# Causal mask products first in the score banks, q and k features one step apart, and modulation dots in the first halves of the down stages

## The chip, the cores and the metric

The kernel runs on one core of a Trainium2 chip. The metric is the device time of one execution in microseconds (us). Before the change the median of three runs is 1501.16 us (1500.08 to 1504.64).

The core has five engines that run side by side and wait for each other by semaphores: PE (matrix products into PSUM banks; its weight loads are listed apart as PEld), DVE and ACT (element-wise work), POOL and SP (here they mostly issue DMAs).

## What is computed

A trunk of two layers over 512 tokens of width 1024, all in f32. In each layer, with `h` the normalised and modulated input:

```python
mod = c_act @ w_ada + b_ada                      # shifts, scales and gains of both halves
h = rmsnorm(x, norm1_w) * (1 + sc1) + sh1
u = h @ w_in                                     # pool, conv, q, k, v and three gates
merged = gate0 * (pool(u) @ p_pool) + gate1 * (conv(u) @ p_conv) + gate2 * (attn(q, k, v) @ p_attn)
x = x + g1 * (merged @ w_out)
h2 = rmsnorm(x, norm2_w) * (1 + sc2) + sh2
x = x + g2 * ((silu(h2 @ w_gate) * (h2 @ w_up)) @ w_down)
```

The attention has 8 heads of 64 with normalised q and k and a partial rotation. Keys lie in two blocks of 256. A query sees the causal part of its own block, and queries of the second block see the first block unless its gate rules it out.

## The kernel before, in words

**Products in three passes.** Every f32 operand is split into a high part and a rest (`split_w` for weights, L320 to L330, ACT line L325 and DVE line L328; `split_from` for activations, L504 to L513). A product is three matrix products, high x high, high x rest, rest x high (`mm3`, L157). `matmul`, `transpose` and all that is wrapped in `pin` keep the program's order on their engine; the rest of ACT's and DVE's work is put in order by the framework's planner.

**The clock of the program.** `mm3` counts the columns of main products. Every 2048 columns (four `mm3` of 512) it calls `tick` (L133): each fiber (a generator) whose count has run out goes one step further, and then `run_bulk` adds `bulk_rate` to a credit that is capped at 4.0 and runs queued side tasks as long as the credit isn't negative, each taking its cost off.

**Weights.** They arrive by SP's queue as raw tiles, in the order in which they are used (`load_w`, `next_w`; usually four chunks ahead, two in the second half of a down stage).

**Attention** (L645) is a fiber. For each of four head pairs it transposes and splits the q and the k features (`to_features`, L563: four transposes into one of the four PSUM banks with tag `mm`, then ACT L511 and DVE L512), both in one step, and starts four units, one for each block of 128 queries. A unit (L574) makes the scores of two heads in a PSUM tile `pair` (three passes, and the causal mask as a product of an identity with a bf16 mask, added after the first pass), the softmax (DVE L592 to L617, ACT L595 to L612), and some steps later the transposes of the probabilities (L624) and the product with v (L631), which is copied by ACT L637 and DVE L638. The gate products of the layer run meanwhile; the first product that needs the attention's result stands 56.5 steps after the conv products at which the fiber is queued.

**Norms.** `Norm.stat` sums squares by a product with ones; `newton` (L463) makes the reciprocal root: an ACT approximation (L467) and one Newton step in four DVE instructions (L468 to L471). It is called for halves of 256 columns, twice for each of three norms. `apply` then writes the tiles that the next products read (L479, L481, L482).

**Feed-forward.** It goes in four parts (`PARTS`, L47). In a part, hidden columns are computed singly or as pairs of columns by `glu_pair` (L1028), which saves products by sums of weight blocks. The sums are made by POOL's accumulating DMAs (L254, L256) and by DVE (L262, L263) in tiles of tag `w4`, of which there are six; a pair holds four. Each part ends in a down stage: eight output tiles of `nk` `mm3` each, added to x by L937.

**Modulation.** The vector c times `w_ada` is not made on PE. Each 128 outputs are one DMA of 512 KB (`ada_step`, L393, the load L395) and one DVE instruction with an accumulator (`ada_dot`, L371). The 16 dots that the second layer needs first are queued as side tasks at the end of the first part's GLU pairs (L1104), at a cost of 1.2 each, and their tiles are of tag `w4` too.

Of the kernel before, what the change touches and what calls it, by code (L numbers as in the profile page):

```python
# [17 lines left out]
ALU = mybir.AluOpType  # L18
# [3 lines left out]
P = 128  # L22
D = 1024
S = 512
L = 2
KT = D // P
# [12 lines left out]
EPS = 1e-6  # L39
# [38 lines left out]
def hybrid_trunk(ctx, tc, xT, ws, ada, cols, pool_w, qk_w, crow, pos, con, out):  # L78
    nc = tc.nc
    V, A, T = nc.vector, nc.scalar, nc.tensor  # L80
# [17 lines left out]
    def tmp():  # L98
        return work.tile([P, S], F32, tag="tmp", name=nm("tmp"), bufs=5)

    def ps_mm():
        return psum.tile([P, S], F32, tag="mm", name=nm("mm"), bufs=4)

    def ps_pair():
        return psum.tile([P, 2, S], F32, tag="pair", name=nm("pair"), bufs=2)
# [14 lines left out]
    bulk_rate, credit = [0.0], [0.0]  # L120
# [27 lines left out]
    def matmul(*a, **k):  # L148
        tc.keep_in_program_order(T.matmul(*a, **k))  # L149
# [48 lines left out]
    ident16 = const.tile([P, P], BF16, name="ident16")  # L198
# [240 lines left out]
    class Norm:  # L439
# [23 lines left out]
        def newton(self, lo, hi, bank):  # L463
            n = hi - lo
            ss = bank[:, lo:hi]
            y, v, t = tmp(), tmp(), tmp()
            A.activation(y[:, :n], ss, AF.Abs_reciprocal_sqrt, bias=epst, scale=1.0 / D)  # L467
            V.tensor_scalar(v[:, :n], ss, 1.0 / D, EPS, op0=ALU.mult, op1=ALU.add)  # L468
            V.tensor_mul(t[:, :n], v[:, :n], y[:, :n])
            V.scalar_tensor_tensor(t[:, :n], t[:, :n], -0.5, y[:, :n], op0=ALU.mult, op1=ALU.mult)  # L470
            V.scalar_tensor_tensor(self.rstd[:, lo:hi], t[:, :n], 1.5, y[:, :n],  # L471
                                   op0=ALU.add, op1=ALU.mult)
            self.y = y
# [100 lines left out]
    def unit(hp, i, q, k, v, y, nrq, prq):  # L574

        w = P * (i + 1)
        wm = max(w, BLOCK)
        s = ps_pair()
        for z, (qa, ka) in enumerate(((0, 0), (0, 1), (1, 0))):
            for a in range(2):  # L580
                r = slice(a * HD, (a + 1) * HD)
                matmul(s[:, a, :wm], q[qa][r, i * P:(i + 1) * P], k[ka][r, :wm],
                       start=(z == 0), stop=(z == 2))
            if z == 0:
                for a in range(2):
                    matmul(s[:, a, i * P:w], ident16, mask, start=False, stop=False)
        cell = lambda: sm([P, 2], tag="asm", bufs=16)
        nsc, sc = nrq[:, i, 2 * hp:2 * hp + 2], prq[:, i, 2 * hp:2 * hp + 2]
        m, nb, den = cell(), cell(), cell()
        pr = [tmp() for _ in range(2)]  # L590
        if w <= BLOCK:
            V.tensor_reduce(m, s[:, :, :w], axis=AX.X, op=ALU.max)  # L592
            V.tensor_mul(nb, m, nsc)
            for a in range(2):
                A.activation(pr[a][:, :w], s[:, a, :w], AF.Exp, bias=nb[:, a:a + 1],  # L595
                             scale=sc[:, a:a + 1], accum_out=den[:, a:a + 1])
        else:

            gs, pen, mp, nbp, d2 = cell(), cell(), cell(), cell(), cell()
            V.tensor_reduce(gs, s[:, :, :BLOCK], axis=AX.X, op=ALU.add)  # L600
            V.tensor_mul(gs, gs, sc)
            V.tensor_scalar(pen, gs, NEG * BLOCK * SCALE, NEG, op0=ALU.is_lt, op1=ALU.mult)
            V.tensor_reduce(mp, s[:, :, :BLOCK], axis=AX.X, op=ALU.max)
            V.tensor_add(mp, mp, pen)
            V.tensor_reduce(m, s[:, :, BLOCK:w], axis=AX.X, op=ALU.max)
            V.tensor_max(m, m, mp)
            V.tensor_mul(nb, m, nsc)
            V.tensor_add(nbp, nb, pen)
            for a in range(2):
                A.activation(pr[a][:, :BLOCK], s[:, a, :BLOCK], AF.Exp, bias=nbp[:, a:a + 1],  # L610
                             scale=sc[:, a:a + 1], accum_out=den[:, a:a + 1])
                A.activation(pr[a][:, BLOCK:w], s[:, a, BLOCK:w], AF.Exp, bias=nb[:, a:a + 1],  # L612
                             scale=sc[:, a:a + 1], accum_out=d2[:, a:a + 1])
            V.tensor_add(den, den, d2)
        V.reciprocal(den, den)
        for a in range(2):
            V.tensor_scalar(pr[a][:, :w], pr[a][:, :w], den[:, a:a + 1], None, op0=ALU.mult)  # L617
        yield WAIT[i]
        ph, pl = w4([P, i + 1, 2, P], F32R), w4([P, i + 1, 2, P], F32R)
        for aa in ([0, 1],) if i < 2 else ([0], [1]):  # L620
            tp = ps_mm().rearrange("p (j a q) -> p j a q", a=len(aa), q=P)[:, :i + 1]
            for a in aa:
                for j in range(i + 1):
                    transpose(tp[:, j, a - aa[0], :], pr[a][:, j * P:(j + 1) * P], ident)  # L624
            dst = (slice(None), slice(None), slice(aa[0], aa[-1] + 1))
            A.activation(ph[dst], tp, AF.Copy)  # L626
            V.tensor_sub(pl[dst], tp, f32(ph)[dst])
        yield 2
        po = ps_mm()
        for j in range(i + 1):  # L630
            mm3(po[:, :2 * P], cut(v[hp // 2][j // 2], slice(None), j % 2, slice(hp % 2 * P, (hp % 2 + 1) * P)),  # L631
                (ph[:, j].rearrange("p a q -> p (a q)"), pl[:, j].rearrange("p a q -> p (a q)")),
                j == 0, j == i, main=False)
        c = slice(i * P, (i + 1) * P)
        for a in range(2):
            r = slice(a * HD, (a + 1) * HD)
            A.activation(y[0][r, c], po[r, a * P:(a + 1) * P], AF.Copy)  # L637
            V.tensor_sub(y[1][r, c], po[r, a * P:(a + 1) * P], f32(y[0])[r, c])  # L638
# [6 lines left out]
    def attention(l, qk, v, nrq, prq, y_attn):  # L645

        for hp in range(PAIRS):
            q, k = to_features(l, qk, 0, hp), to_features(l, qk, 1, hp)
            y = bigt(), bigt()
            y_attn.append(y)  # L650
            yield 2
            for i in range(TT):
                start(unit(hp, i, q, k, v, y, nrq, prq))
                if i < TT - 1:
                    yield GAP[i]
            yield 1
# [45 lines left out]
    for l in range(L):  # L702
# [371 lines left out]
        for part, (along, single, pairs) in enumerate(PARTS):  # L1074
            act = []
            nk = along + single + 2 * pairs
            if along:
                held = {}
                for n, (k, lo, hi) in enumerate(HALVES + REST):
                    if n == 1:  # L1080
                        second(norm, l, 1, bank)
                        table(AF.Silu, norm.y[:, 0:1])
                    if k not in held:
                        held[k] = next_w()
                    for z in range(2 * FA):
                        mm3(f_ps[z][:, lo:hi], wblk(held[k], z), cut(norm.k(k), slice(None), slice(lo, hi)),
                            k == 0 and lo == 0, k == KT - 1)
                    if k >= HK:
                        make_forms(k - HK)
                del held  # L1090
                for z in range(FA):
                    glu(f_ps[z], f_ps[FA + z])
            for _ in range(single):
                wg = next_w()
                g = ps_mm()
                feature_tile(g, wg)
                u = ps_mm()
                feature_tile(u, next_w())
                glu(g, u)
            bulk_rate[0] = 0.0  # L1100
            for _ in range(pairs):
                glu_pair()
            if part == 0 and l + 1 < L:
                bulk.extend(ada_tasks(l + 1, (SC1, SH1)))  # L1104
            bulk_rate[0] = 0.75
            blk = Blocks(nk, 4)
            if part + 1 < len(PARTS):
                for n in range(KT):
                    o = ps_mm()
                    for k in range(nk):  # L1110
                        mm3(o, blk(n, k), act[k], k == 0, k == nk - 1)
                    residual(n, o, 0, S, G2)
            elif l + 1 == L:
                tail(lambda k: act[k], blk, G2, nk, None, True)
            else:
                flush_bulk()
                drain()
                n1 = Norm()
                table(AF.Abs_reciprocal_sqrt, f32(act[-1][1])[:, 0:1])
                scratch = ps_pair()  # L1120
                bank = scratch[:, 1]
                tail(lambda k: act[k], blk, G2, nk, n1, False, lead(n1, l + 1, 0, bank), 4)
                norm = n1
# [100 lines left out]
```

## Time and profile before

| What | Value |
|---|---|
| median of the runs | 1501.16 us |
| profiled execution, time | 1503.53 us |
| profiled execution, span of its instructions | 1501.7 us |
| mean granted clock of PE | 0.997 |
| HBM read | 213.65 MB |
| POOL busy | 105.6 us, 7% |

The profile is one execution. A line of the trace names the engine, the line of the kernel (L149 is the helper that records all products, so there one goes by tiles), the operation, and what is written and read (`mm<-big,whi`). A line of waits says which engine stood idle, at which of its lines, until which engine's which line was done: total, number of times, longest.

### The profile page before, as it was taken

Reading aid. Unit: us, or ns where it says so; the run is one execution under the profiler, and the core shown is the slowest. Engines: PE = TensorE matmul, PEld = TensorE weight load, DVE = VectorE, ACT = ScalarE, POOL = GpSimd, SP = SyncE. Lnnn points to the kernel's source line nnn. Section 1 sums busy time; section 2 is a strip of 40 time slices with the busy share of each in tenths; the row PEclk is TensorE's granted clock in tenths of the full one; section 3 lists DMA queues with packets and bytes.
Section 4 is the critical chain, followed back from the end, with each engine's and each line's share of the span. In section 5 each row is a group of like instructions: output and inputs, shape, how many; then the busy total and the mean of one; then the engine's idle time right before and its main releaser. Section 6 shows DMA issues by size and latency. Waiting matters only on the chain.

```text
span 1501.7 us, 22027 instructions
## 1 busy us (share of the span) xinstructions
PE 1478.1 (98%) x8523; PEld 1282.1 (85%) x8523; DVE 1042.0 (69%) x1797; ACT 657.7 (44%) x1138; POOL 105.6 (7%) x157
## 2 busy tenths in 40 slices
PE   9999999999999999999999999999999999999999
PEld 7887777788889898989988877777888889989997
DVE  7876777756586766767575678776666847757672
ACT  4634444433364352535444344554335534525350
POOL 0000000010000220310000000001000102211200
PEclk9999999999999999999999999999999999999999
DMA  9523434483226775644333244346721445727431
GB/s 343 194 85 140 155 128 140 146 237 130 64 99 210 216 185 175 175 114 133 107 104 100 98 155 140 134 133 187 226 82 53 126 141 148 199 80 195 137 99 71
DMA packets 84409, 217.20 MB, mean 145 GB/s; under 512 B 10832, under 2 KB 23760, under 8 KB 84304
## 3 DMA queue, kind: packets, MB, share of 16 engines
q1 hardware_dynamic: 67456, 177.37, 35.1%
q0 software_dynamic: 16128, 37.76, 11.4%
q8 instruction: 67, 1.10, 0.3%
q10 hardware_dynamic: 720, 0.66, 0.1%
q14 instruction: 38, 0.31, 0.1%
HBM read 213.65 MB, written 2.10 MB: 144 GB/s over the span
## 4 chain that ended last, share of the span: by engine, by line
PE 83%; DVE 6%; DMA 5%; ACT 3%; issue 2%; SPq 1%; POOL 0%; DVEq 0%; ACTq 0%; POOLq 0%
PE mm L149 70%; PE pair L149 11%; DMA raw<-in_ws 2%; DVE wlo L328 2%; PE mm L155 2%; DMA w<-in_ada 1%; ACT whi L325 1%; DMA w<-in_ws 1%; DVE w L371 1%; DVE raw L371 1%; SPq L232 0%; ACT tmp L610 0%; DMA x<-in_xT 0%; DMA raw<-in_ada 0%; ACT tmp L612 0%
## 5 line engine op out<-in xcount | busy, mean ns | idle before, releaser
L149 PE MATMUL mm<-big,whi 128*128 128x512 f32 (+1 forms) x4362 | 1085.7, 340 | 11.3 <-DVE tmp L1059 5.1
L149 PEld LDWEIGHTS mm<-big,whi 128*128 128x128 f32 x4362 | 748.6, 190 | 101.7 <-DVE tmp L1059 6.9
L149 PE MATMUL mm<-big,wlo 128*128 128x512 f32 (+1 forms) x2181 | 738.2, 338 | 0.0
L149 PEld LDWEIGHTS mm<-big,wlo 128*128 128x128 f32 x2181 | 415.1, 190 | 44.4
L325 ACT ACTIVATE whi<-raw 128x1024 fp32r<-128x1024 f32 (+2 forms) x240 | 248.9, 1039 | 334.9 <-PE mm L149 272.5
L328 DVE TENSOR_TENSOR wlo<-raw,whi 128x1024 fp32r<-128x1024 f32 (+2 forms) x240 | 285.7, 1195 | 121.5 <-ACT whi L325 116.2
L937 DVE SCALAR_TENSOR_TENSOR x<-mm,mod,x 128x512 f32<-128x512 f32 (+1 forms) x90 | 62.2, 691 | 121.5 <-PE mm L149 121.4
L325 ACT ACTIVATE whi<-w 128x1024 fp32r<-128x1024 f32 x72 | 76.2, 1058 | 148.9 <-PE mm L149 116.9
L254 POOL DMA_DIRECT2D w<-in_ws x72 | 45.5, 642 | 1027.1 <-issue 267.4
L328 DVE TENSOR_TENSOR wlo<-w,whi 128x1024 fp32r<-128x1024 f32 x72 | 86.8, 1222 | 30.5 <-ACT whi L325 29.8
L371 DVE SCALAR_TENSOR_TENSOR raw<-raw,csil 128x1024 f32<-128x1024 f32 x64 | 78.0, 1221 | 4.7 <-DMA raw<-in_ada 4.4
L149 PE MATMUL pair<-whi,big 128*128 128x512 f32 x224 | 76.8, 390 | 0.0
L149 PE MATMUL pair<-big,whi 128*128 128x256 f32 (+1 forms) x376 | 74.0, 295 | 0.0
L256 POOL DMA_DIRECT2D w<-in_ws x72 | 64.5, 920 | 131.7 <-DMA w<-in_ws 124.0
L149 PEld LDWEIGHTS pair<-big,whi 128*128 128x128 f32 x376 | 60.4, 191 | 2.2
L149 PE MATMUL mm<-whi,big 128*128 128x512 f32 x160 | 57.2, 394 | 1.7 <-ACT big L495 1.4
L149 PE MATMUL pair<-big,wlo 128*128 128x256 f32 (+1 forms) x188 | 55.4, 295 | 0.0
L509 DVE TENSOR_TENSOR big<-tmp,big 128x512 fp32r<-128x512 f32 x48 | 33.0, 691 | 24.9 <-ACT big L508 23.9
L149 PEld LDWEIGHTS pair<-whi,big 128*128 128x128 f32 x224 | 42.1, 188 | 8.6
L626 ACT ACTIVATE w<-mm 128x512 fp32r<-128x512 f32 (+2 forms) x48 | 24.0, 525 | 46.5 <-PE mm L155 46.5
L149 PE MATMUL pair<-wlo,big 128*128 128x512 f32 x112 | 43.7, 390 | 0.0
L371 DVE SCALAR_TENSOR_TENSOR w<-w,csil 128x1024 f32<-128x1024 f32 x32 | 38.5, 1222 | 5.7 <-DMA w<-in_ada 5.6
(185 smaller groups left out, 1265.6 us busy)
## 6 DMA issues: line engine op xcount, KB each, us to landing
raw<-in_ws SPq DMA_DIRECT2D x146, 512.0 KB, 3.4
w<-in_ws POOLq DMA_DIRECT2D x144, 256.0 KB, 5.0
raw<-in_ada SPq DMA_DIRECT2D x64, 512.0 KB, 3.4
w<-in_ada SPq DMA_DIRECT2D x32, 512.0 KB, 5.1
raw<-in_ws SPq DMA_DIRECT2D x64, 256.0 KB, 3.8
raw<-in_ws SPq DMA_DIRECT2D x24, 384.0 KB, 3.1
raw<-in_ws SPq DMA_DIRECT2D x16, 448.0 KB, 5.2
raw<-in_ws SPq DMA_DIRECT2D x36, 128.0 KB, 2.8
```

The source lines that it names most:

```text
L149: tc.keep_in_program_order(T.matmul(*a, **k))
L155: tc.keep_in_program_order(T.transpose(*a))
L254: nc.gpsimd.dma_start(dst, self.source(0, 1))
L256: nc.gpsimd.dma_start(dst, self.source(*other), accum_op=ALU.add)
L325: A.activation(hi[:, :n], raw[:, :n], AF.Copy)
L328: ins = V.tensor_sub(lo[:, :n], raw[:, :n], f32(hi)[:, :n])
L371: return V.scalar_tensor_tensor(aw, aw, 1.0, csil, op0=ALU.mult, op1=ALU.mult, accum_out=mod[l][:, part, j:j + 1])
L509: V.tensor_sub(lo, src, f32(hi))
L626: A.activation(ph[dst], tp, AF.Copy)
L937: V.scalar_tensor_tensor(x[k][:, lo:hi], src, mod[l][:, part, k:k + 1], x[k][:, lo:hi], op0=ALU.mult, op1=ALU.add)
```

## The change

Four edits. In `newton` the term `ss / D + EPS` is no longer made by an instruction of its own: three DVE instructions stand in place of four, and the first reads the PSUM bank and ACT's result. In `unit` the two mask products come first in the banks and start them, and all three score passes add to them. In `attention` the k features are made one step after the q features, so each head pair takes 12 steps in place of 11. In the down stages the credit rate is 1.5 a step in the first four of eight output tiles, and 0 in the last four of all parts but the last, where it was 0.75 throughout; only the first layer's down stages have tasks queued.

```diff
@@ -463,11 +463,10 @@
         def newton(self, lo, hi, bank):
             n = hi - lo
             ss = bank[:, lo:hi]
-            y, v, t = tmp(), tmp(), tmp()
+            y, t = tmp(), tmp()
             A.activation(y[:, :n], ss, AF.Abs_reciprocal_sqrt, bias=epst, scale=1.0 / D)
-            V.tensor_scalar(v[:, :n], ss, 1.0 / D, EPS, op0=ALU.mult, op1=ALU.add)
-            V.tensor_mul(t[:, :n], v[:, :n], y[:, :n])
-            V.scalar_tensor_tensor(t[:, :n], t[:, :n], -0.5, y[:, :n], op0=ALU.mult, op1=ALU.mult)
+            V.scalar_tensor_tensor(t[:, :n], ss, D * EPS, y[:, :n], op0=ALU.add, op1=ALU.mult)
+            V.scalar_tensor_tensor(t[:, :n], t[:, :n], -0.5 / D, y[:, :n], op0=ALU.mult, op1=ALU.mult)
@@ -576,14 +575,14 @@
         s = ps_pair()
+
+        for a in range(2):
+            matmul(s[:, a, i * P:w], ident16, mask, start=True, stop=True)
         for z, (qa, ka) in enumerate(((0, 0), (0, 1), (1, 0))):
             for a in range(2):
                 r = slice(a * HD, (a + 1) * HD)
                 matmul(s[:, a, :wm], q[qa][r, i * P:(i + 1) * P], k[ka][r, :wm],
-                       start=(z == 0), stop=(z == 2))
-            if z == 0:
-                for a in range(2):
-                    matmul(s[:, a, i * P:w], ident16, mask, start=False, stop=False)
+                       start=False, stop=(z == 2), skip_group_check=True)
@@ -645,7 +644,9 @@
         for hp in range(PAIRS):
-            q, k = to_features(l, qk, 0, hp), to_features(l, qk, 1, hp)
+            q = to_features(l, qk, 0, hp)
+            yield 1
+            k = to_features(l, qk, 1, hp)
@@ -1102,10 +1103,12 @@
             if part == 0 and l + 1 < L:
                 bulk.extend(ada_tasks(l + 1, (SC1, SH1)))
-            bulk_rate[0] = 0.75
+            bulk_rate[0] = 1.5
             blk = Blocks(nk, 4)
             if part + 1 < len(PARTS):
                 for n in range(KT):
+                    if n == KT // 2:
+                        bulk_rate[0] = 0.0
                     o = ps_mm()
```

## Prediction

> **What bounds the kernel now.** I read the page first: the shares of the engines, then who PE waits for, then PE's own starts in the stretches that the change touches.
>
> ```profile
> span 1501.7 us, 22027 instructions
> ## 1 busy us (share of the span) xinstructions
> PE 1478.1 (98%) x8523; PEld 1282.1 (85%) x8523; DVE 1042.0 (69%) x1797; ACT 657.7 (44%) x1138; POOL 105.6 (7%) x157
> ```
>
> PE is busy for 98% of the span and takes its instructions in the program's order, so only two things can move the time: the pace at which PE issues, and the 24 us in which it stands still. The profiled execution took 1503.5 us with a span of 1501.7, so 1.8 us lie around it; it is 2.4 us above the median of the three runs, 1501.16. The sum below is made against 1503.5. The waits of PE, longest in total first:
>
> ```profile
> PE mm L155 <- DVE tmp L617: 5.1, 4, 2.0
> PE mm L149 <- DVE tmp L1059: 5.1, 9, 2.9
> PE mm L149 <- DVE big L512: 2.8, 4, 1.4
> PE mm L149 <- ACT big L481: 2.4, 2, 1.2
> ```
>
> L617 ends the normalisation of an attention unit, L1059 is in a GLU pair, L512 splits q and k features, L481 is the first normalised tile after the Newton step. All three subjects of the change stand in this list, and the mask stands in none: its cost is hidden in PE's pace.
>
> **Part 1, mask products first.** One unit (the fourth kind, 512 columns), PE in order of time: start, length, what.
>
> ```profile
> 901.07 0.39 PE L149 MATMUL mm<-big,wlo 128*128 128x512 f32 x1
> 901.39 0.50 PE L149 MATMUL pair<-big,big 64*128 64x512 f32 x2
> 901.82 0.28 PE L149 MATMUL pair<-mask,ident 128*128 128x128 bf16 x2
> 902.03 0.73 PE L149 MATMUL pair<-big,big 64*128 64x512 f32 x4
> 902.70 0.88 PE L155 MATMUL mm<-ident,tmp 128*128 128x128 f32 x6
> ```
>
> A score pass is two products on 64 rows each, which run together. From the product ahead to pass 1: 0.32 us. From pass 1 to the mask: 0.43. The two mask products until pass 2: 0.21. Passes 2 and 3 until the transposes: 0.67, so 0.33 each. A full-height product of 512 columns otherwise makes way after 0.23:
>
> ```profile
> 177.70 5.47 PE mm L149 x24
> ```
>
> ```profile
> L149 PEld LDWEIGHTS <-ident 128*128 128x128 bf16 x64 | 3.6, 97 | 5.5 <-issue 3.4
> ```
>
> (5.47/24 = 0.228 us.) So the switch from full height to 64 rows costs 0.09 over the pace, and the switch from 64 rows back to the mask 0.10 over a pass (0.43 against 0.33), about the 97 ns of the mask's weight load, which starts only with its product.
>
> With the mask first, the row of steps is: product ahead to mask (X), mask to pass 1 0.21, then three passes of 0.33. The same instructions are issued; the saving is 0.32 + 0.43 - 0.33 - X = 0.42 - X. X isn't in the trace in this form. If the mask's weights are loaded under the product ahead, X is about the pace, 0.23; if they stand open, 0.23 + 0.097 = 0.32. The nearest row is the same switch to another full-height identity product, the transposes of q and k:
>
> ```profile
> 949.10 0.39 PE L149 MATMUL mm<-big,wlo 128*128 128x512 f32 x1
> 949.33 1.03 PE L155 MATMUL mm<-ident,w 128*128 128x128 f32 x8
> 951.76 0.50 PE L149 MATMUL mm<-big,whi 128*128 128x512 f32 x1 [1.40 <-DVE big L512]
> ```
>
> There X is 0.23, so I take it: 0.42 - 0.23 = 0.19 (0.184 with the pace unrounded). The mask row counts 64 loads, two a unit: 32 units. 32 x 0.184 = **-5.9 us**; ends: -2.9 (X = 0.32) and -6.1 (X = 0.225). Nothing hides it: PE itself gets shorter. The wait for q and k, and for the bank, stays where it is, ahead of the unit.
>
> The Trainium skill, "TensorE: Matmul & The Clock Gate", Part 3, The mechanism, speaks against this: a weight load is to overlap running products only where its row group differs. By it the mask's full-height load could not hide under a full-height product, and the part would give 2.9 us. The trace disagrees for other full-height loads (24 products at 0.228 us, each with a load of 0.19 of its own), but no run here shows it for the mask's type.
>
> **Part 2, q and k features one step apart.** A step is 2048 columns of main products, 12 x 0.227 = 2.7 us of PE. The rows of 949 show today's price: q's and k's eight transposes fill two of the four mm banks at once, the next product needs one of them back, and DVE comes to L512 late. PE's waits for L512 are the 2.8 us above. With the step between, q's bank has 2.7 us more until the next but one is asked for; k's transposes (0.44 us of PE), its ACT and DVE split (0.67 and 0.75) move by one step. No DMA moves with them. Gone then: between 0 and 2.8. The ring of four banks is asked as often, since k now meets the output of a unit in the same step, so I take three quarters, -2.1.
>
> Against it: the transposes of a fourth unit used to stand behind the next pair's first scores and now stand ahead of them.
>
> ```profile
> 260.30 0.38 PE L149 MATMUL pair<-big,big 64*128 64x256 f32 x2
> ...
> 261.26 1.09 PE L155 MATMUL mm<-ident,tmp 128*128 128x128 f32 x8
> ```
>
> ```profile
> 259.96 0.88 DVE L617 TENSOR_SCALAR tmp<-tmp,asm 128x512 f32<-128x512 f32 x2
> ```
>
> The normalisation ends at 260.84, the transposes start at 261.26: 0.42 us to spare, of which the scores fill 0.96. Without them this unit waits 0.5. Six units have a next pair; bounds 0 and 6 x 0.96 = 5.8; most have more to spare, so I take one more such unit, +1.0. **Part 2: -1.1 us**, ends -2.8 and +5.8. Four added steps also put the last unit's output at step 55 of the 56.5 that stand ahead of the first product with y_attn. What that product would wait for:
>
> ```profile
> 1050.07 1.59 PE L149 MATMUL mm<-w,big 128*128 128x256 f32 x12
> ```
>
> ```profile
> 1052.62 0.29 DVE L638 TENSOR_TENSOR big<-mm,big 64x128 fp32r<-64x128 f32 x1 [0.34 <-ACT big L637]
> ```
>
> The copies end 1.25 us after the output. After it 1.5 steps (4.1 us) are left, and three of that product's four terms come first: cost 0, and if DVE were busy for longer than that, the rest of its delay.
>
> **Part 3, the dots.** By the code's credit (4 at the start of a down stage, 1.2 a dot), the first down stage of layer 0 issues 4 dots in step 1 and 11 in its twelve steps now, 10 in its first six with the change; the second takes 6 in place of 5. The dots themselves aren't the limit, their tiles are:
>
> ```profile
> L371 DVE SCALAR_TENSOR_TENSOR w<-w,csil x11: 1218/1224/1227, 474.5 to 503.3; 128x1024 f32<-128x1024 f32 x11
> ```
>
> ```profile
> DMA to landing us min/median/max: 3.2/4.4/6.6
> ```
>
> ```profile
> 497.22 1.22 DVE L371 SCALAR_TENSOR_TENSOR w<-w,csil 128x1024 f32<-128x1024 f32 x1 [2.03 <-DMA w<-in_ada]
> ...
> 500.36 1.22 DVE L328 TENSOR_TENSOR wlo<-raw,whi 128x1024 fp32r<-128x1024 f32 x1
> 501.50 1.22 DVE L371 SCALAR_TENSOR_TENSOR w<-w,csil 128x1024 f32<-128x1024 f32 x1
> ...
> 504.44 0.75 DVE L937 SCALAR_TENSOR_TENSOR x<-mm,mod,x 128x512 f32<-128x512 f32 x1
> ```
>
> (The first row is the eleven dots of that stage, the second the landing of all 16 loads, the rest DVE at the stage's end.) Two w tiles are free for them, so two dots go every 5.6 us (a landing of 4.4 and a dot of 1.2). The ninth already waits for its DMA until 497.2 and can't come sooner. The tenth, loaded right behind, would run at 498.7 in place of 501.5, and there is no eleventh (at 503.3 now). So the tiles come free at 498.4 and 499.9, not at 502.7 and 504.5. What hangs on that (POOL, DVE, and two windows with length, busy time of PE, PEld, DVE, ACT and POOL, granted clock, DMA):
>
> ```profile
> 503.29 0.57 POOL L254 DMA_DIRECT2D w<-in_ws  x1 [47.22 <-DVE w L371]
> ```
>
> ```profile
> 505.11 3.48 DVE L328 TENSOR_TENSOR wlo<-w,whi 128x1024 fp32r<-128x1024 f32 x3
> ...
> 519.41 0.69 DVE L262 TENSOR_TENSOR w<-w,raw 128x512 f32<-128x512 f32 x1 [3.23 <-DMA w<-in_ws]
> ```
>
> ```profile
> 521.30:524.70 3.40, 0.63 (x5) 0.64 (x6) 3.04 (x6) 2.37 (x4) 0.43 (x1) 1.00 1.08 266
> 524.70:528.10 3.40, 3.40 (x18) 3.40 (x18) 2.87 (x5) 1.36 (x3) 1.55 (x3) 0.51 0.86 198
> ```
>
> POOL's sums for the second GLU pair wait for a dot's tile, land late, DVE stands still 3.23 us in L262 with L1059 queued behind it, and PE loses 2.9 us at L1059; after the window with 0.63 of 3.40 us busy the granted clock is 0.51 for 3.4 us, another 1.7. With the chain 4.3 us earlier at its start, and at least 2.5 in its second half, which runs over the three L328 (they can follow at 502.5, when the split of 500.36 is done behind the last dot), I take -2.7 for the wait and -1.7 for the clock: **-4.4 us**, ends 0 and -4.6. The denser loads pass SP's queue ahead of raw weights, and the split of 500.36 now stands behind all dots, at 501.3. Its weights are the GLU pair's, and the down stage before it lasts until 504.4 (the last L937), so 1.9 us cover it; were loads to take 3 us longer for a pair of dots, PE would lose about that.
>
> **Part 4, Newton.** One DVE instruction less in each of six. It matters only in the two where PE waits for L481:
>
> ```profile
> 400.99 0.42 DVE L468 TENSOR_SCALAR tmp<-pair 128x256 f32<-128x256 f32 x1
> ```
>
> ```profile
> 403.16 0.84 ACT L325 ACTIVATE whi<-raw 128x768 fp32r<-128x768 f32 x1 [2.21 <-PE mm L149]
> 403.91 0.49 ACT L481 ACTIVATE big<-tmp,mod 128x256 fp32r<-128x256 f32 x1
> ```
>
> DVE's chain gets about 0.42 shorter (the product that replaces it reads the same bank), but L481 stands in ACT's queue behind L325, which waits for PE. So **0**; if L481 came ahead of L325, at most its 0.84 each, -1.7 in all.
>
> **Sum:** -5.9 - 1.1 - 4.4 - 0 = -11.4, from 1503.5: 1492.1. The median run is 2.4 lower; if what it lacks is the clock drop, 9.7 come off it, 1491.5, and if it has the drop, 1489.8. I say **1491**.
>
> **Rivals.**
> 1. The mask's weight load stays open (X = 0.32): 3 us less, 1494. For: it is open now behind 64 rows. Against: the q/k transposes.
> 2. The banks' wait only moves, from q's and k's tiles to k's and the output's: -2.1 is lost, 1493. For: same four banks, DVE no freer; against: fewer asked for at once.
> 3. The dots don't get earlier: they run at the pace of two tiles whatever the credit says, and the tenth keeps its place behind L262 and L328. Then part 3 is 0: 1495.4. For: the ninth waits for DMA already; against: the last two dots came without a wait.
> 4. Slower: the shifted units meet DVE at worse moments, and L617 becomes the bound. Now 4 of the 16 third and fourth units wait, 1.28 us on the mean. If all 16 did, 12 x 1.28 = +15.4: 1506. It decides from about twelve more such units, each of which has to lose its slack first; that of the unit at 261.26 was only 0.42, which speaks for it, while the added step thins out DVE's work by a twelfth, which speaks against.
>
> **Chances.** Forecast 0.52 (1487 to 1495); rival 1 0.13, rival 2 0.13, rival 3 0.09, two of them together 0.05 (1498), rival 4 0.08. About 0.3%, 4.5 us, is what a measurement of this kernel can tell from no change, so faster means under 1496.7 and slower over 1505.7. Rivals 1 to 3 spill over 1496.7 with 0.03, 0.03 and 0.04, the pair with all: faster 0.77, same 0.16, slower 0.07. The range reaches from 1485 (all of 2.8 without the loss beside it, which is 1.7 more, Newton's 1.7, and another clock drop less) to 1499 (two rivals together).
>
> **What would show it.** Right: mask 0.23 after the product ahead and 32 units shorter by 0.18; no 3.2 us idle at L262 before the first pair's L1059, POOL's L254 near 498.5; L512 below 1 us among PE's waits. Wrong: a mask start 0.32 after the product ahead; a dot after 500 in the first down stage; L617's waits grown beyond 8 us.

## The result and the profile after

The changed kernel takes 1485.7 us in the median of four runs (1481.1 to 1487.2), beside 1502.3 for before on the same chip: a ratio of 0.9884, interval 0.9856 to 0.9911. Timed again later it gave 0.9869 (0.9847 to 0.9890). So it is 17 to 20 us faster; 10 were forecast, and 0.9884 of the 1501.16 shown then is 1483.7, just below the range that was given.

The profiled execution took 1481.1 us. Its span, and the busy time of its engines (us, share of the span, instructions):

```profile
span 1479.3 us, 22041 instructions
PE 1464.6 (99%) x8523; PEld 1276.7 (86%) x8523; DVE 1039.0 (70%) x1791; ACT 659.7 (45%) x1138; POOL 105.7 (7%) x157
```

PE issues the same 8523 products and is busy for 13.5 us less. Its waits (engine, its line, engine and line waited for, total, times, longest; L1060 is L1059 of before, and L616, L511, L480 and L481 each stand one lower than there):

```profile
PE mm L155 <- ACT whi L325: 2.6, 2, 1.7
PE mm L149 <- DVE tmp L1060: 2.2, 8, 0.3
...
PE mm L149 <- DVE big L481: 0.9, 4, 0.3
...
PE mm L149 <- ACT big L480: 0.4, 2, 0.2
PE mm L155 <- DVE big L511: 0.3, 1, 0.3
...
PE mm L155 <- DVE tmp L616: 0.2, 1, 0.2
```

The score waits (L617 and L512, 7.9 us) are down to 0.5, with 2.6 new ones at the units' transposes put down to L325 (whether that split was last there, or the unit's own normalisation beside it, the trace doesn't settle). The GLU wait lost 2.9, the Newton wait 1.1.

PE's own pace, a unit of 512 columns, first after:

```profile
934.27 0.39 PE L149 MATMUL mm<-big,wlo 128*128 128x512 f32 x1
934.50 0.28 PE L149 MATMUL pair<-mask,ident 128*128 128x128 bf16 x2
934.71 0.96 PE L149 MATMUL pair<-big,big 64*128 64x512 f32 x6
935.61 0.66 PE L155 MATMUL mm<-ident,tmp 128*128 128x128 f32 x4
```

From the product ahead to the transposes it is 935.61 - 934.27 = 1.34 us; before it was 902.70 - 901.07 = 1.63. The mask comes 0.23 behind the product ahead, as predicted, but the unit is 0.29 shorter, not 0.18. The same shows when the busy time of all products that write the score banks is summed over the two attention stretches (length; busy of PE, PEld and, on the score tiles, DVE and ACT). Before:

```profile
sum 375.00, PE 37.22 PEld 15.49 DVE 38.90 ACT 52.96; mean PE 18.61 PEld 7.75 DVE 19.45 ACT 26.48
```

After:

```profile
sum 375.00, PE 30.75 PEld 14.26 DVE 38.38 ACT 52.50; mean PE 15.37 PEld 7.13 DVE 19.19 ACT 26.25
```

This is 6.5 us less in PE busy time (overlapped ends count once there; by starts it is 32 x 0.29 = 9.3).

The dots. POOL's first sum for the second GLU pair, and then the window in which that pair's products run (busy time of PE, PEld, DVE, ACT and POOL; granted clock; DMA):

```profile
489.96 0.57 POOL L254 DMA_DIRECT2D w<-in_ws  x1 [43.42 <-DVE w L371]
```

```profile
510.00:513.40 3.40, 3.40 (x31) 3.40 (x30) 3.23 (x5) 3.25 (x6) 1.42 (x2) 1.00 1.05 342
```

The stage's first dot starts at 465.0, at 474.5 in before, so 489.96 answers to 499.5 on the old scale, 3.8 us ahead of the 503.29 of before (498.5 was predicted). PE no longer stands still at L1060 for longer than 0.3 us, and the clock of 0.51 behind it is gone.

Added up against the profile of before (1503.5 to 1481.1, 22.4 us): 9.3 by the units' pace, 4.8 by the attention's waits (7.9 to 3.1), 2.9 at the GLU pair, 1.1 at Newton, and some 3.2 because this execution has no drop of the granted clock where before has two, behind the waits that end at 162.39 and at 524.07. That is 21.3 of the 22.4. The runs in the middle of after's four have a mean granted clock of 0.999, this one of 1.000, so they will have some drop: the experiments with several runs are weighed by ratios, not by this one execution.

### The profile page after: what moved, and what is told of

Its sections match the earlier page's. It is cut to its first block, busy times and chain, and to the rows that moved or that the text cites. A ratio compares the mean times of both kernels' runs of the same rounds, so it can differ in the third digit from the quotient of the medians.

```text
span 1479.3 us, 22041 instructions
## 1 busy us (share of the span) xinstructions
PE 1464.6 (99%) x8523; PEld 1276.7 (86%) x8523; DVE 1039.0 (70%) x1791; ACT 659.7 (45%) x1138; POOL 105.7 (7%) x157
## 4 chain that ended last, share of the span: by engine, by line
PE 90%; DVE 5%; ACT 2%; DMA 2%; issue 1%; SPq 0%; DVEq 0%; ACTq 0%
PE mm L149 77%; PE pair L149 11%; PE mm L155 2%; DVE wlo L328 1%; ACT whi L325 1%; DMA raw<-in_ws 1%; DVE raw L371 1%; DMA w<-in_ada 0%; ACT tmp L611 0%; ACT tmp L609 0%; DMA x<-in_xT 0%; DVE w L371 0%; DVE tmp L1060 0%; SPq L232 0%; DVE asm L599 0%
## 5 line engine op out<-in xcount | busy, mean ns | idle before, releaser
L325 ACT ACTIVATE whi<-raw 128x1024 fp32r<-128x1024 f32 (+2 forms) x240 | 248.9, 1039 | 312.8 <-PE mm L149 249.4
L325 ACT ACTIVATE whi<-w 128x1024 fp32r<-128x1024 f32 x72 | 76.2, 1058 | 147.4 <-PE mm L149 100.5
L508 DVE TENSOR_TENSOR big<-tmp,big 128x512 fp32r<-128x512 f32 x48 | 33.0, 691 | 24.2 <-ACT big L507 23.2
```

Source lines behind the costliest of these rows:

```text
L325: A.activation(hi[:, :n], raw[:, :n], AF.Copy)
L508: V.tensor_sub(lo, src, f32(hi))
```

## The experiments

### Each part alone

Theory A was the accounting above, part by part. The rivals were the terms of the prediction. Four kernels, each before with one part. The mask first:

```diff
+        for a in range(2):
+            matmul(s[:, a, i * P:w], ident16, mask, start=True, stop=True)
...
-                       start=(z == 0), stop=(z == 2))
-            if z == 0:
-                for a in range(2):
-                    matmul(s[:, a, i * P:w], ident16, mask, start=False, stop=False)
+                       start=False, stop=(z == 2), skip_group_check=True)
```

> Before with the first part alone: the mask's products ahead of the three score passes. Theory A (the gain is local to each unit, and the second pass-to-pass step is cheap): the product ahead to the mask 0.23, pass to pass 0.22 to 0.33 for the first step and 0.11 to 0.23 for the second, 0.29 less in each of 32 units, so 9.2 to 9.3 us less in PE's own pace, and the waits of PE at L617 and L512 may stay. Theory B (the prediction's step): both pass-to-pass steps 0.33 in a unit of four tiles, 0.184 less a unit, 5.9 us less in all. In the profile of the changed kernel the second step was 0.11 to 0.23, so A is expected here; the open question is whether the mask alone also takes the waits of DVE with it (then 11 us or more) or only makes them longer, because the units come closer together (then 7 to 8 us).

Measured: ratio 0.9974 (0.9960 to 0.9987), 3.9 us (2.0 to 6.0). Every unit is as short as in after (the fourth kind 1339 ns from the product ahead to the transposes, 1627 before), so A holds for PE's pace, and yet of the 9.3 only 3.9 arrive. The waits grew:

```profile
PE mm L155 <- DVE tmp L617: 7.1, 4, 2.3
...
PE mm L149 <- DVE big L512: 4.4, 3, 2.1
```

From 7.9 to 11.5, so 3.6 of the 9.3 are given back at once. More went to the clock. One of these waits and the two windows around it:

```profile
907.29 1.22 PE L149 MATMUL mm<-big,whi 128*128 128x512 f32 x2 [2.09 <-DVE big L512]
```

```profile
904.30:907.70 3.40, 1.31 (x5) 0.79 (x4) 3.30 (x8) 2.20 (x9) 0.00 (x0) 0.92 0.22 61
907.70:911.10 3.40, 3.40 (x14) 2.82 (x14) 3.14 (x8) 1.95 (x5) 0.00 (x0) 0.58 0.38 142
```

PE is busy for 1.31 of 3.40 us, and in the next window, fully busy, its clock is 0.58. These windows aren't cut where the clock changes: it is 0.50 from 907.14 to 910.55, so PE loses half of 3.41, 1.7 us. This profile has five such drops, before has two. Two of the three more lie in the attention and cost some 1.7 each. The third lies in the start (19.7 us), where the 200th product comes 0.4 us later than in before. There remain 9.3 - 3.6 - 3.8 = 1.9; the spans of the two profiles differ by 2.1. The shorter unit alone runs into VectorE.

Then q and k one step apart:

```diff
-            q, k = to_features(l, qk, 0, hp), to_features(l, qk, 1, hp)
+            q = to_features(l, qk, 0, hp)
+            yield 1
+            k = to_features(l, qk, 1, hp)
```

> Before with the second part alone: the features of q and k one step apart. Theory A (the step itself takes the waits away): PE's waits at L617's tile (5.1 us in before) and at L512's (2.8 us) nearly vanish and the time falls by 3 to 6 us. Theory B (the prediction's step): only most of L512's 2.8 go, 1.0 comes back in the fourth units, and the time falls by 1.1 us; L617's waits stay near 5. Theory C: alone the step does nothing, within 1 us of before, and the waits went only because part one came with it.

Measured: 0.9967 (0.9952 to 0.9982), 5.0 us: A, and not the 1.1 of the prediction. Its waits:

```profile
PE mm L155 <- ACT whi L325: 1.9, 1, 1.9
...
PE mm L155 <- DVE tmp L617: 0.6, 1, 0.6
...
PE mm L155 <- DVE big L512: 0.2, 1, 0.2
```

Some of it is given back: beside the 1.9 at L325, the waits at L508 and L509, at two places behind the attention, come to 1.8 and 1.0, 0.2 each in before.

The dots in the first half of the stage:

```diff
-            bulk_rate[0] = 0.75
+            bulk_rate[0] = 1.5
...
+                    if n == KT // 2:
+                        bulk_rate[0] = 0.0
```

> Before with the third part alone: next layer's modulation dots at rate 1.5 in the first half of a down stage and none in its second. Both theories price it at 4.4 to 4.6 us: no idle time of 3.2 us on POOL ahead of L262, POOL's L254 near 498.5 to 499.5, the wait of 2.7 us at L1059 gone, and the drop of the granted clock behind it with it. If it gives 2.7 only, the drop of the clock came from elsewhere; if it gives nothing, the wait moved.

Measured: 0.9963 (0.9952 to 0.9975), 5.6 us (3.8 to 7.2). POOL's first sum, and the GLU wait of this kernel, 5.1 in before:

```profile
496.21 0.57 POOL L254 DMA_DIRECT2D w<-in_ws  x1 [41.89 <-DVE w L371]
```

```profile
PE mm L149 <- DVE tmp L1059: 2.1, 8, 0.3
```

The dots of this profile begin 2.0 us earlier than before's (472.5 against 474.5), so the 496.21 answers to 498.2, and 498.5 was predicted. Between the 900th product and the 2700th PE gains 4.6 us on before. The price of 4.4 holds. The wait of 3.23 us ahead of the second pair's L262 (on VectorE) is gone: L262 runs at 514.11 without one.

And the shorter Newton step:

```diff
-            V.tensor_scalar(v[:, :n], ss, 1.0 / D, EPS, op0=ALU.mult, op1=ALU.add)
-            V.tensor_mul(t[:, :n], v[:, :n], y[:, :n])
-            V.scalar_tensor_tensor(t[:, :n], t[:, :n], -0.5, y[:, :n], op0=ALU.mult, op1=ALU.mult)
+            V.scalar_tensor_tensor(t[:, :n], ss, D * EPS, y[:, :n], op0=ALU.add, op1=ALU.mult)
+            V.scalar_tensor_tensor(t[:, :n], t[:, :n], -0.5 / D, y[:, :n], op0=ALU.mult, op1=ALU.mult)
```

> Before with the fourth part alone: one VectorE instruction less in each Newton step. Theory A: the planner's order on ACT turns round where it did in the changed kernel (the group's activation ahead of L325), the wait of 2.4 us behind it falls to about 1.3, and both layers together give 1.5 us. Theory B (the prediction's step): it stays behind L325, and the gain is 0 to 0.4. Either lies below about 0.3% of the time, so the verdict is read from the waits in the profile.

Measured: 0.9990 (0.9976 to 1.0004), so the time can't tell. ACT's order can (L480 is L481 of before):

```profile
404.18 0.51 ACT L480 ACTIVATE big<-tmp,mod 128x256 fp32r<-128x256 f32 x1 [1.93 <-DVE tmp L478]
404.59 0.83 ACT L325 ACTIVATE whi<-raw 128x768 fp32r<-128x768 f32 x1
```

The activation now stands ahead of L325. The waits behind it are 0.9 at L481 and 0.4 at L480, 1.3 in place of 2.4: A by the order, though 1.1 us and not 1.5.

### The first two parts together

The first two of these edits in one kernel:

```diff
+        for a in range(2):
+            matmul(s[:, a, i * P:w], ident16, mask, start=True, stop=True)
...
+            yield 1
+            k = to_features(l, qk, 1, hp)
```

> Before with the first and the second part together. Alone they gave ratios of 0.9974 and 0.9967, 3.9 and 5.0 us. Theory A (the mask's 9.2 us of shorter units were partly lost again in longer waits of PE at L617 and L512 and in the drops of the granted clock behind them, and the step between q and k takes these away): together more than the sum, 11 to 14 us, L617 and L512 below 1 us in all, and fewer drops of the clock than the mask alone has. Theory B (the two add up): 8.9 us. Theory C (they pay for the same waits): 5 to 7 us.

Measured: 0.9912 (0.9897 to 0.9926), 13.2 us, where the two alone give 3.9 and 5.0. A: the second part also pays the first one out. In the attention PE waits for L617 and L512 for 0.5 us in all, and no window there has a lower clock. What remains moved on:

```profile
PE mm L149 <- DVE tmp L1061: 7.7, 9, 5.6
```

PE now comes earlier to the GLU pair whose sums wait for the dots, and stands there for 5.6 us in place of 2.9. The third part therefore has more to remove from this profile than alone. The times don't show that: by the ratios the third and the fourth part add 4.2 to 6.5 us to the 13.2, and alone they gave 5.6 and 1.5.

### Where the 0.29 of a unit lies

After, with the mask's products behind the third pass:

```diff
-        for a in range(2):
-            matmul(s[:, a, i * P:w], ident16, mask, start=True, stop=True)
...
-                       start=False, stop=(z == 2), skip_group_check=True)
+                       start=(z == 0), stop=False)
+        for a in range(2):
+            matmul(s[:, a, i * P:w], ident16, mask, start=False, stop=True)
```

> After with the mask's products behind the third score pass. Theory A (of two passes that follow one another without a full-height product between them, only the first step after a full-height product costs 0.22 to 0.33, every later one 0.11 to 0.23, wherever the mask stands): the first pass 0.32 behind the product ahead, then 0.22 and 0.11 (units of two tiles), 0.28 and 0.17 (three), 0.33 and 0.23 (four). Theory B (the cheap step comes only behind the mask's products, whose type is another): 0.22 and 0.22, 0.28 and 0.28, 0.33 and 0.33. In both the switch back to the mask costs 0.31 to 0.43 as in before, so that the unit is longer than in after by about 0.2 (A) or 0.3 (B), and the kernel by 6 to 10 us.

Measured: 1480.6 us in a single run. Both theories were wrong on the sum: the mask behind costs nothing against the mask ahead. Its fourth kind of unit:

```profile
204.73 0.39 PE L149 MATMUL mm<-big,wlo 128*128 128x512 f32 x1
205.04 0.96 PE L149 MATMUL pair<-big,big 64*128 64x512 f32 x6
205.94 0.29 PE L149 MATMUL pair<-mask,ident 128*128 128x128 bf16 x2
206.06 0.83 PE L155 MATMUL mm<-ident,tmp 128*128 128x128 f32 x6
```

1.33 us, as in after. Step by step in a unit of two tiles, each from the last product of one pass to the first of the next, in ns: the first pass 318 behind the product ahead, the second pass 220 behind the first, the third 113 behind the second, the mask 207 behind the third. In before the mask came 313 behind the first pass, and 217 lay between the last two. So the slow step is always the one behind the *first* pass after a full-height product, whatever follows it: about 0.1 us. This gave theory D: an excursion from 128 rows to 64 and back costs a fixed 0.29 us (0.09 on entering, 0.10 on the step behind its first pass, 0.09 to 0.10 on leaving); before makes two a unit, the mask between the passes making the second one. The next kernel, again an edit of after, puts it between the second pass and the third.

```diff
-        for a in range(2):
-            matmul(s[:, a, i * P:w], ident16, mask, start=True, stop=True)
...
+            if z == 1:
+                for a in range(2):
+                    matmul(s[:, a, i * P:w], ident16, mask, start=False, stop=False)
```

> After with the mask's products between the second and the third pass. Theory D, formed on the mask-last run (an excursion from full-height products to the 64-row passes has a fixed price of about 0.29 us, of which 0.107 falls on the step behind its first pass, whatever comes next; before has two excursions a unit, the changed kernel and the mask-last one have one): first pass to second 0.22 (units of two tiles), second pass to mask 0.21 and not 0.31, third pass to transposes 0.31 and not 0.205, the unit as long as in before, and the kernel some 9 us above after: 1491 to 1497. Theory E (only the place beside the first pass costs): the unit of after plus at most 0.1, the kernel 1484 to 1490.

```profile
207.72 0.39 PE L149 MATMUL mm<-big,wlo 128*128 128x512 f32 x1
208.04 0.73 PE L149 MATMUL pair<-big,big 64*128 64x512 f32 x4
208.70 0.29 PE L149 MATMUL pair<-mask,ident 128*128 128x128 bf16 x2
208.92 0.50 PE L149 MATMUL pair<-big,big 64*128 64x512 f32 x2
209.35 0.87 PE L155 MATMUL mm<-ident,tmp 128*128 128x128 f32 x6
```

1.63 us, the unit of before, and 1493.4 us in a single run. In a unit of two tiles the mask comes 205 to 210 ns behind the second pass and the transposes 310 to 315 behind the third: D. The busy time of its score products over the same two stretches, which is 30.85 in the mask-last kernel:

```profile
sum 375.00, PE 37.31 PEld 15.48 DVE 38.42 ACT 52.50; mean PE 18.66 PEld 7.74 DVE 19.21 ACT 26.25
```

So it isn't "first" that pays but "not in between".

The rows of the weight loads point to a reason for the step behind the first pass. In the unit of after that starts at 934.27, the loads of the first pass start with its products (934.71). Those of the second and of the third pass are these:

```profile
934.82 0.19 PEld L149 LDWEIGHTS pair<-big,big 64*128 64x128 f32 x2
935.05 0.19 PEld L149 LDWEIGHTS pair<-big,big 64*128 64x128 f32 x2
```

Both passes follow their loads by 0.23 us (935.05 and 935.28). But the second's loads start 0.11 behind the first pass's products, the third's together with the second's products. In before the 0.1 is there too, though the mask follows and its load starts only with its own product (901.82). So it may be that the first pass itself starts late, behind weights that are loaded in the open; no run here tests that.

### What the added step does, and what its place

After, with both features in one step and the added step behind them:

```diff
-            q = to_features(l, qk, 0, hp)
+            q, k = to_features(l, qk, 0, hp), to_features(l, qk, 1, hp)
             yield 1
-            k = to_features(l, qk, 1, hp)
```

> After with q's and k's features in one step again, and the added step behind both, so that a pair of heads still takes as many steps. Theory A (the added step itself gives VectorE and ScalarE the time, whichever of the two features it stands beside): the time of after within 2 us, L616's waits below 1 us. Theory B (q and k must not ask for two banks in one step): L511's waits come back with 2 to 4 us, and the time is 3 to 6 us above after.

Measured: 0.9908 (0.9887 to 0.9928), by the ratios 3.6 to 5.9 us above the two measurements of after.

```profile
PE mm L149 <- DVE big L511: 4.6, 4, 1.8
...
PE mm L155 <- DVE tmp L616: 0.2, 1, 0.2
```

Each theory is right for one wait. The twelfth step, wherever it stands, takes away the wait for the normalisation (L616: 0.2 us). Only the place between q and k takes away the wait for their split (L511: 4.6 here, 0.3 in after).

### When the last dot lets go of its tile

After, with the dots at rate 1.5 through the whole down stage:

```diff
-                    if n == KT // 2:
-                        bulk_rate[0] = 0.0
```

> After with the dots' rate of 1.5 kept through the whole down stage. Theory A (what counts is when the last dot's tile comes free, because POOL's sums take the tiles behind it): more dots are issued in the second half, at 5.6 us for two they end 5 to 15 us later than the tenth does in after, POOL's L254 moves by as much, the idle time at L262 and the wait of PE at L1060 come back, and the time is 3 to 10 us above after. Theory B (it is enough that the first ten come early): the waits of after, within 1 us of it.

Measured: 1498.7 us in a single run, 13 to 15 above the medians of after, more than A gave, and the wait lies elsewhere (at L1060 it stays at 0.3 us). All 16 dots run in the stage, and POOL's sum comes at 505.72, 15.8 us later than in after:

```profile
L371 DVE SCALAR_TENSOR_TENSOR w<-w,csil x16: 1218/1224/1227, 465.5 to 507.5; 128x1024 f32<-128x1024 f32 x16
```

```profile
506.40 1.22 DVE L328 TENSOR_TENSOR wlo<-raw,whi 128x1024 fp32r<-128x1024 f32 x1
```

```profile
507.67 0.58 PE L149 MATMUL pair<-big,wlo 128*128 128x256 f32 x1 [11.14 <-DVE wlo L328]
```

The split of the raw weights for the GLU pair stands on VectorE behind dots that wait for their DMA. In after it starts at 492.62, here at 506.40, and PE waits 11.1 us for it, with a clock of 0.5 for another 5.4 us (to 513.08). The 11.1 and half of the 5.4 make 13.8 us, about the whole loss. That is the cover of 1.9 us that the prediction named for the split, broken. So at a rate of 1.5 the zero in the second half is needed, because of DVE's queue. What POOL's later sum would cost by itself can't be seen behind this wait, and a lower rate in the second half, 0.75 as in before, was not run.

### Two versions that might beat both

The changed kernel was timed again beside them, without an edit.

> The changed kernel itself, timed again beside the others of this call. Expected: the ratio 0.988 to 0.990 to before, as in its first measurement.

Measured: 0.9869 (0.9847 to 0.9890), 1483.6 us.

A third unit with one step more before its transposes:

```diff
-    WAIT = (2, 3, 3, 3)
+    WAIT = (2, 3, 4, 3)
```

> After with one step more between the scores and the transposes of a third unit. Theory A (the 2.6 us that PE waits at L155 in layer 1's third units, put down to L325, come from a probability tile that is ready late, and a later start hides them): 1 to 3 us faster than after, these waits gone. Theory B (the four score and output steps then fall together with the fourth unit's, and the wait moves to L616 or to the mm banks): the same time or up to 3 us slower.

Measured: 0.9961 (0.9947 to 0.9975), 13 us slower than after: slower as in B, and far beyond its bound. Its longest wait, and ACT's order ahead of it:

```profile
PE mm L149 <- ACT big L893: 4.0, 1, 4.0
```

```profile
943.12 1.06 ACT L325 ACTIVATE whi<-raw 128x1024 fp32r<-128x1024 f32 x1 [4.23 <-PE mm L149]
944.21 0.56 ACT L609 ACTIVATE tmp<-pair,asm,nrq 128x256 f32<-128x256 f32 x1
...
947.70 0.63 ACT L893 ACTIVATE big<-mm 128x512 f32<-128x512 f32 x1
```

ACT stands idle for 4.23 us at a weight split that waits for PE, and then come a unit's exponentials, and behind them the copy L893 that PE waits for. In after a split that waits (1.97 us) stands there too, but L893 comes ahead of the exponentials (940.56 and 941.03). One step moved by hand changes the planner's order somewhere else. In all PE stands idle for 24.2 us, 16.3 in the second profile of after, and the clock is low for three stretches of 3.41 us in place of one, 3.4 us more. That is the 11.3 us by which these two spans differ.

The scores of a pair's first two units side by side, the mask ahead in the first and behind in the second:

```diff
-    GAP = (2, 3, 3, 3)
-    WAIT = (2, 3, 3, 3)
+    GAP = (0, 3, 3, 3)
+    WAIT = (2, 4, 3, 3)
...
+        if i != 1:
+            for a in range(2):
+                matmul(s[:, a, i * P:w], ident16, mask, start=True, stop=True)
...
+        if i == 1:
+            for a in range(2):
+                matmul(s[:, a, i * P:w], ident16, mask, start=False, stop=True, skip_group_check=True)
...
-            yield 2
+            yield 3
...
-                if i < TT - 1:
-                    yield GAP[i]
+                if i < TT - 1 and i > 0:
+                    yield GAP[i] + (i == 1)
```

> After with the scores of each pair's first two units side by side, the mask ahead in the first and behind in the second, so that both share one excursion to the 64-row passes; the first unit comes one step later, the second's scores one step earlier. Theory D (an excursion has a fixed price of 0.29 us): eight excursions fewer, 2.3 us faster than after (ratio to before 0.985 to 0.987), if no engine comes late. Rival: the two units ask VectorE and ScalarE at once, PE's waits at L155 and L149 in the attention grow by more than 2.3 us, and the time is that of after or up to 8 us above.

```profile
180.62 0.28 PE L149 MATMUL pair<-mask,ident 128*128 128x128 bf16 x2
180.83 0.97 PE L149 MATMUL pair<-big,big 64*128 64x256 f32 x12
181.74 0.28 PE L149 MATMUL pair<-mask,ident 128*128 128x128 bf16 x2
181.83 1.43 PE L149 MATMUL mm<-w,big 128*128 128x256 f32 x10
```

```profile
sum 375.00, PE 28.66 PEld 13.77 DVE 38.23 ACT 51.86; mean PE 14.33 PEld 6.89 DVE 19.12 ACT 25.93
```

Measured: 0.9850 (0.9824 to 0.9876), 1481.1 us. Twelve products run in one excursion, and the score products are busy for 2.1 us less than in after, as D has it for eight excursions less (2.3). The ratio lies where D put it; its interval overlaps that of after, so the profile shows the gain and the time alone does not.

## Why the prediction was too small

The direction was right, and so were the mechanisms of the dots and of the two features' banks. In the other terms a step failed, and the sum came out 7 to 10 us too small.

1. **Mask.** X, the step from the product ahead to the mask, was taken as 0.23 and is 0.23. Rival 1 falls: behind a full-height product the mask's load costs nothing over the pace (0.230 us for 512 columns). With it falls the 2.9 us that would follow from the rule of the Trainium skill, "TensorE: Matmul & The Clock Gate", Part 3, that a weight load overlaps running products only where its row group differs. That the mask's load hides as those of the f32 products do isn't shown: it starts 4 ns ahead of its product (934.49), theirs 0.22 us ahead (934.04 for the product at 934.27). The step that failed is "then three passes of 0.33": after the change only the first of the two steps between passes is 0.33, the second is 0.23. The trace of before couldn't show a second step, since the mask cut its three passes into one and two. Nor is the 0.10 ahead of the mask the price of the mask's load, as the prediction had it: behind a second pass the mask comes without it. So 0.184 a unit should have been 0.29, 9.3 in place of 5.9 by PE's starts.
2. **Features.** The step that failed is the +1.0 for fourth units that lose their slack, together with leaving L617's 5.1 us out of what can go. L617 was put as a risk only (rival 4); in truth the twelfth step takes its wait nearly away (0.6 in the kernel with this part alone), as the kernel with the step elsewhere shows too. With it goes the first of before's two drops of the clock, which follows one of these waits. The -2.1 of L512 was right (2.5 of 2.8). Alone the part gives 5.0 (2.7 to 7.2), not 1.1. Rivals 2 and 4 fall.
3. **Dots.** -4.4 was predicted, 4.6 is found between the same products, and POOL's sum, the vanished idle time at L262 and the clock came as described. Rival 3 falls.
4. **Newton.** The step that failed is "L481 stands in ACT's queue behind L325". The planner let it pass. The waits fall by 1.1, within the bound of 1.7; the time alone can't tell it from 0.

What the sum also missed is that the parts don't add: the mask's shorter units are worth 3.9 us alone and, by the difference of the ratios, 8.2 once the added step is there (13.2 - 5.0). The intervals of the three ratios, some 2 us each way, make this difference of 4.3 only just clear of noise; the waits, 11.5 us at L617 and L512 with the mask alone and 0.5 with both, say the same. The prediction summed the first two as if each met the waits of before.

## What to carry to other kernels

Count the changes between full-height products and products on part of the rows, not the products: each excursion had a fixed price here (0.29 us), so a lone full-height product among half-height ones is best moved to either end. When PE's own pace gets shorter, the gain arrives only if the engines that feed it have slack in the same period; look at the waits before and buy the slack in the same edit. And price a wait of 1.5 us or more at more than its length, because the clock can drop behind it (up to 1.7 us each time here).

## What the runs showed of the hardware

The granted clock falls without PE being idle for a whole window. In before a wait of 1.47 us (160.92 to 162.39) was enough (two windows: length, busy time of PE, PEld, DVE, ACT and POOL, granted clock, DMA):

```profile
159.50:162.90 3.40, 1.93 (x14) 1.11 (x14) 1.48 (x6) 1.90 (x8) 0.00 (x0) 1.00 0.39 141
162.90:166.30 3.40, 3.40 (x12) 2.72 (x10) 2.76 (x7) 1.69 (x3) 0.00 (x0) 0.50 0.03 5
```

In the mask-only kernel it fell with PE busy for 1.31 of 3.40 us (then 0.58). In the changed kernel, timed again, a wait of 2.35 us at a unit's transposes did it too (0.62 from 893.10 to 896.50):

```profile
891.81 1.08 PE L155 MATMUL mm<-ident,tmp 128*128 128x128 f32 x6 [2.35 <-ACT whi L325]
```

The same place with a wait of 1.71 us, in the first profile of after, had no drop. The Trainium skill, "TensorE: Matmul & The Clock Gate", Part 1, puts the fall behind at least one idle window of some 3.4 us; and the return behind a busy one of the same length; the low stretch of about one window agrees with that, the full idle window does not.

The length of the wait alone doesn't decide. The 1.47 us above were enough, and 1.96 us ahead of the transposes at 1043.70 in the same profile were not. In each profile the falls lie a whole number of 3.413 us apart (162.92 and 524.74 in before, 106 times that), which fits that a wait counts by what falls into one such stretch. Busy time in the stretch isn't all that counts either: behind 1040.15 to 1043.56 in before, PE busy for 1.59 us, the clock stayed, and behind 159.51 to 162.92, busy for 1.94, it fell. What decides stays open. So does the cause of the 0.1 us behind the first half-height pass: the runs show where it falls, and only the loads' rows hint at why.
